# An empty first turn and six branches in TensorE's loop of a batched matmul

## The chip, the cores and the metric

One core of one Trainium2 chip. The metric is the device time of one execution in microseconds.

Each ratio is the mean time of one kernel's runs over that of the other's runs of the same rounds, so it is not quite the ratio of the medians quoted beside it.

## The reference

```python
b1, b2, m, k, n = 8, 16, 256, 512, 384      # 128 independent products
x      = randn(b1, b2, m, k)   # float32
weight = randn(b1, b2, k, n)   # float32
out    = np.matmul(x, weight).astype(np.float32)
```

## The kernel before

The 128 batches go in 32 groups of four (`NG = 32`, `G = 4`). Each engine has its own loop, and the loops meet only through counting semaphores. SyncE issues all loads and stores. ScalarE casts x to bf16 and copies results out of PSUM. VectorE casts the weights and copies the transposed x out of PSUM. TensorE transposes x, then multiplies. `BIAS` is added to some counters at the start, so that a wait for an earlier group never asks for a value of zero or less.

```python
XS, WS, OS = 2, 2 * G // D, 4      # two groups of x and of weights in SBUF
BS, TS, WBS = 1, 2, 2 * G
PT, PO = 4, 2                      # PSUM buffers
BIAS = 8

def load(e, t, U, s):              # SyncE; group n
    n = t * U + s
    if not isinstance(n, int) or n >= XS:
        e.wait_ge(x_cast, n + (1 - XS))          # slot of x free
    e.dma_start(x_sb[s % XS][:], ...).then_inc(x_in[s % XS], 16)
    for d in range(G // D):
        ...
        e.wait_ge(w_cast, n * (G * S) + ((d + 1) * D * S - 2 * G * S))
        e.dma_start(w_sb[slot][:], ...).then_inc(w_in[slot], 16)

def multiply(e, t, U, s):          # TensorE; group n
    n = t * U + s
    e.wait_ge(x_cast, n + 1)
    for q in range(T):             # 4 x 4 transposes
        e.wait_ge(t_copied, n * T + (q + 1 - PT + BIAS))
        ... transposes ...
        ins.then_inc(t_made, 1)
    e.wait_ge(w_cast, n * (G * S) + G * S)
    for q in range(T):             # 4 x 32 multiplies
        e.wait_ge(t_copied, n * T + (q + 1 + BIAS))
        e.wait_ge(o_copied, n * T + (q + 1 - PO + BIAS))
        ... multiplies ...
        ins.then_inc(p_made, 1)

@block.tensor
def _(e):
    U = 2
    e.sem_inc(t_made, BIAS)
    e.sem_inc(p_made, BIAS)
    e.wait_ge(id_done, 2)
    with e.Fori(0, NG // U) as t:   # 16 turns of two groups
        for s in range(U):
            multiply(e, t, U, s)
# ... (cut: SyncE's, VectorE's, ScalarE's and GpSimd's programs)
```

## Time and profile before

| | before |
|---|---|
| time, median of 4 runs | 519.98 us (519.65 to 520.08) |
| bytes over HBM | 167.77 MB read, 50.33 MB written |
| DMA rate between 230 and 262 us | 428 GB/s, DMA share 1.01 |
| PE, VectorE, ScalarE busy | 61%, 62%, 41% of the span |

The table is read from below: no engine is busy for two thirds of the time, and the transfers run at one even rate from the second slice of the span to the last but one. The lines that carry this are shown in the prediction. Two more lines are needed to compare with later. The timeline of the kernel before: start in us, duration in us, engine, line, operation, and in brackets the idle time before it and what ended it.

### The profile page before, as it was taken

What the parts mean: (1) busy time and instruction counts of PE and PEld (TensorE: products, weight loads), DVE (VectorE), ACT (ScalarE), POOL (GpSimd) and SP (SyncE); (2) the same over time, 40 slices, a digit from 0 to 9 for tenths busy, and PEclk for the clock granted to TensorE, in tenths of its full rate; (3) what the DMA queues carried; (4) which work ended last, traced back from release to release, by engine and by line L of the source; (5) the groups of instructions that cost most, each with busy time, mean ns of one, the idle gap of its engine ahead of it and who ended that gap; (6) DMA issues with size and microseconds to landing.
All of it is one profiled execution on the core that took longest, in us unless ns stands there. A gap on an engine that the chain in (4) does not pass through costs nothing.

```text
span 518.3 us, 11239 instructions
## 1 busy us (share of the span) xinstructions
PE 315.5 (61%) x4608; PEld 198.8 (38%) x4608; DVE 323.9 (62%) x384; ACT 212.7 (41%) x193; POOL 0.7 (0%) x6
## 2 busy tenths in 40 slices
PE   0686773576655675655756557665567665675653
PEld 0455452343433443433424334343344333443331
DVE  0878867655577555775556765557755577555670
ACT  3065462454234553245542445423454324553242
POOL 0000000000000000000000000000000000000000
PEclk9988788877687778678776877778787868886787
DMA  8999999999999999999999999999999999999995
GB/s 332 431 426 426 427 427 429 430 426 429 430 428 429 431 426 428 428 431 431 425 429 429 430 430 429 427 428 429 430 430 428 426 431 430 429 428 427 428 431 214
DMA packets 18868, 218.16 MB, mean 421 GB/s; under 512 B 2096, under 2 KB 2096, under 8 KB 2608
## 3 DMA queue, kind: packets, MB, share of 16 engines
q1 hardware_dynamic: 18864, 218.11, 99.2%
q8 instruction: 2, 0.03, 0.0%
q14 instruction: 2, 0.02, 0.0%
HBM read 167.77 MB, written 50.33 MB: 421 GB/s over the span
## 4 chain that ended last, share of the span: by engine, by line
DMA 81%; DVE 12%; issue 2%; PE 2%; ACT 1%; SPq 0%; DVEq 0%; ACTq 0%
DMA w_sb<-in_weight_dram 81%; DVE w_bf L148 12%; PE po L181 2%; ACT x_bf L130 0%; DVEq _compat.py:109 0%; SPq L108 0%; ACT out_sb L195 0%; SPq L100 0%; DVE x_t L154 0%; DVEq L143 0%; DVEq L230 0%; SPq L107 0%; ACTq L194 0%; SPq L288 0%; SPq L54 0%
## 5 line engine op out<-in xcount | busy, mean ns | idle before, releaser
L148 DVE CAST w_bf<-w_sb 64x1536 bf16<-64x1536 f32 x256 | 244.5, 955 | 179.4 <-DMA w_sb<-in_weight_dram 166.7
L181 PE MATMUL po<-w_bf,x_t 128*32 128x384 bf16 x4096 | 231.4, 400 | 121.0 <-DVE x_t L154 121.0
L195 ACT COPY out_sb<-po 128x768 f32<-128x768 f32 x128 | 99.2, 802 | 290.2 <-PE po L181 290.2
L181 PEld LDWEIGHTS po<-w_bf,x_t 128*32 128x32 bf16 x4096 | 124.5, 117 | 225.4 <-DVE x_t L154 130.9
L167 PE MATMUL pt<-identity,x_bf 128*128 128x128 f32 x512 | 84.0, 329 | 73.0 <-ACT x_bf L130 73.0
L130 ACT CAST x_bf<-x_sb 128x2048 bf16<-128x2048 f32 x64 | 118.4, 1901 | 6.1 <-DMA x_sb<-in_x_dram 6.1
L167 PEld LDWEIGHTS pt<-identity,x_bf 128*128 128x128 f32 x512 | 74.3, 213 | 84.9 <-issue 84.9
L154 DVE COPY x_t<-pt 128x1024 bf16<-128x1024 bf16 x128 | 79.5, 683 | 1.0
L130 ACT ACT_TABLE_LOAD x1 | 1.3, 1283 | 1.3 <-PEq L237 1.3
masks.py:199 POOL TENSOR_SCALAR_AFFINE_SELECT identity<-identity 128x128 f32<-128x128 f32 x1 | 0.3, 292 | 0.2 <-POOL identity L204 0.2
L204 POOL MEMSET identity<- 128x128 f32 x1 | 0.2, 204 | 0.5 <-SPq L54 0.5
L277 POOL MEMSET const-bfloat16-1.0<- 128x1 bf16 x1 | 0.1, 101 | 0.0
L277 POOL MEMSET const-uint8-127<- 128x1 uint8 x1 | 0.1, 101 | 0.0
L277 POOL MEMSET const-float32-0.0<- 128x1 f32 x1 | 0.1, 98 | 0.2 <-issue 0.2
L277 POOL MEMSET const-float32-1.0<- 128x1 f32 x1 | 0.1, 98 | 0.0
## 6 DMA issues: line engine op xcount, KB each, us to landing
w_sb<-in_weight_dram SPq DMA_DIRECT2D x64, 1536.0 KB, 27.5
x_sb<-in_x_dram SPq DMA_DIRECT2D x32, 2048.0 KB, 25.8
out_dram<-out_sb SPq DMA_DIRECT2D x31, 1536.0 KB, 30.6
out_dram<-out_sb SPq DMA_DIRECT2D x4, 384.0 KB, 3.6
```

Of the source, the lines that this page charges most:

```text
L130: ins = e.copy(out=x_bf[s % BS][:, :, h], in_=x_sb[s % XS][:].rearrange("p r (q s c) -> p r s q c", s=S, c=KO)[:, :, h],)
L148: e.tensor_copy(out=w_bf[(s * G + d * D + a) % WBS][h * HP : (h + 1) * HP], in_=w_sb[slot][a * HP : (a + 1) * HP, h * KO : (h + 1) * KO, : ...
L154: e.tensor_copy(out=x_t[s % TS][:, 2 * q : 2 * q + 2], in_=pt[(s * T + q) % PT][:].bitcast(bf16),).then_inc(t_copied, 1)
L167: ins = e.transpose(pt[(s * T + q) % PT][:, rr, h, :], words[:, 2 * q + rr, h :: KO // 2], identity[:],)
L181: ins = e.matmul(po[(s * T + q) % PO][mine, rr, :N], x_t[s % TS][:, 2 * q + rr, ko // 2, mine, ko % 2], w_bf[(s * G + i) % WBS][:, ko, :], ...
L195: e.copy(out=out_sb[s % OS][:, 2 * q : 2 * q + 2, :], in_=po[(s * T + q) % PO][:, :, :N],).then_inc(o_copied, 1)
L204: e.memset(identity[:], 0.0).then_inc(id_done, 1)
L277: nc = _bacc.Bacc("TRN2", target_bir_lowering=False, num_devices=1)
```

## The change

It looks like a step towards software pipelining: TensorE's body is cut into a part that transposes and two halves that multiply, each under a condition of its own, and the loop gets one more turn at its beginning. Parts of different groups could later be run in one turn. In this step nothing overlaps yet: in turn 0 all six conditions are false, and in turns 1 to 16 all are true. As TensorE's group number is now two too high, the counters that it waits for are raised by two groups (`LEAD`), and the waits of others are shifted by as much.

```diff
-    BIAS = 8
+    BIAS = 16
+    LEAD = 2
 ...
-            e.wait_ge(x_cast, n + (1 - XS))
+            e.wait_ge(x_cast, n + (1 - XS + LEAD))
 ... (the wait for w_cast likewise)
-    def multiply(e, t, U, s):
+    def transpose(e, t, U, s):
 ... (the transposes; their wait shifted by LEAD * T)
+    def multiply(e, t, U, s, q):
 ... (one block q of multiplies; its waits shifted by LEAD * T)
     # VectorE's program
         e.sem_inc(t_copied, BIAS)
+        e.sem_inc(w_cast, LEAD * G * S)
     # TensorE's program
-        e.wait_ge(id_done, 2)
-        with e.Fori(0, NG // U) as t:
+        with e.Fori(0, NG // U + 1) as t:
             for s in range(U):
-                multiply(e, t, U, s)
+                with e.If(t > 0):
+                    if s == 0:
+                        e.wait_ge(id_done, 2)
+                    transpose(e, t, U, s)
+                for h in range(2):
+                    with e.If(t > 0):
+                        for q in range(h * T // 2, (h + 1) * T // 2):
+                            multiply(e, t, U, s, q)
     # ScalarE's program
         e.sem_inc(o_copied, BIAS)
+        e.sem_inc(x_cast, LEAD)
```

More of the change, by code (lines that the diff above doesn't have):

```diff
@@ L106, in load @@
             if not isinstance(n, int) or n >= 2:
-                e.wait_ge(w_cast, n * (G * S) + ((d + 1) * D * S - 2 * G * S))
+                e.wait_ge(w_cast, n * (G * S) + ((d + 1) * D * S + (LEAD - 2) * G * S))
             e.dma_start(
@@ L163, in multiply @@
         for q in range(T):
-            e.wait_ge(t_copied, n * T + (q + 1 - PT + BIAS))
+            e.wait_ge(t_copied, n * T + (q + 1 - PT + BIAS - LEAD * T))
             for rr in range(2):
@@ L172, in multiply @@
             ins.then_inc(t_made, 1)
-        e.wait_ge(w_cast, n * (G * S) + G * S)
-        for q in range(T):
-            e.wait_ge(t_copied, n * T + (q + 1 + BIAS))
-            e.wait_ge(o_copied, n * T + (q + 1 - PO + BIAS))
-            for rr in range(2):
-                for ko in range(KO):
-                    for i in range(G):
-                        mine = slice(i * C, (i + 1) * C)
-                        ins = e.matmul(
-                            po[(s * T + q) % PO][mine, rr, :N],
-                            x_t[s % TS][:, 2 * q + rr, ko // 2, mine, ko % 2],
-                            w_bf[(s * G + i) % WBS][:, ko, :],
-                            start=(ko == 0),
-                            stop=(ko == KO - 1),
-                        )
-            ins.then_inc(p_made, 1)
+    def multiply(e, t, U, s, q):
+        n = t * U + s
+        if q == 0:
+            e.wait_ge(w_cast, n * (G * S) + G * S)
+        e.wait_ge(t_copied, n * T + (q + 1 + BIAS - LEAD * T))
+        e.wait_ge(o_copied, n * T + (q + 1 - PO + BIAS - LEAD * T))
+        for rr in range(2):
+            for ko in range(KO):
+                for i in range(G):
+                    mine = slice(i * C, (i + 1) * C)
+                    ins = e.matmul(
+                        po[(s * T + q) % PO][mine, rr, :N],
+                        x_t[s % TS][:, 2 * q + rr, ko // 2, mine, ko % 2],
+                        w_bf[(s * G + i) % WBS][:, ko, :],
+                        start=(ko == 0),
+                        stop=(ko == KO - 1),
+                    )
+        ins.then_inc(p_made, 1)
     def copy_out(e, t, U, s, q):
```

## The prediction

> **What bounds the kernel now.** I read the page's busy table and its slices first, then the chain of waits, the transfers with their time to landing, the waits of the DMA queue's issuer, and last the timeline of the start, the middle and the end.
>
> ```profile
> span 518.3 us, 11239 instructions
> PE 315.5 (61%) x4608; PEld 198.8 (38%) x4608; DVE 323.9 (62%) x384; ACT 212.7 (41%) x193; POOL 0.7 (0%) x6
> DMA  8999999999999999999999999999999999999995
> HBM read 167.77 MB, written 50.33 MB: 421 GB/s over the span
> DMA 81%; DVE 12%; issue 2%; PE 2%; ACT 1%; SPq 0%; DVEq 0%; ACTq 0%
> ```
>
> No compute engine is busy for two thirds of the span, while the DMA row stands at nine tenths or more in all slices but the first and the last. The chain that ended last is 81% transfer. In the middle (230 to 262 us) the view by stretches gives 428 GB/s at a DMA share of 1.01. The bytes are 167.77 + 50.33 = 218.1 MB; at 428 GB/s they need 509.6 us, and the span is 518.3 us. So some 9 us in the whole kernel are not pure transfer, all at the two ends. The kernel is bound by bytes, and this change moves no byte of data.
>
> How much lateness of TensorE does the transfer stream stand before it runs dry? That is in the time from issue to landing:
>
> ```profile
> w_sb<-in_weight_dram SPq DMA_DIRECT2D x64, 1536.0 KB, 27.5
> x_sb<-in_x_dram SPq DMA_DIRECT2D x32, 2048.0 KB, 25.8
> out_dram<-out_sb SPq DMA_DIRECT2D x31, 1536.0 KB, 30.6
> ```
>
> A load of 1.57 MB takes 3.7 us alone at 428 GB/s, but lands after 27.5 us: the rest is queue ahead of it. An x load finds 25.8 x 0.428 = 11 MB queued, itself included. A group of four batches moves one x load, two weight loads and one store, 2.10 + 2 x 1.57 + 1.57 = 6.8 MB, or 15.9 us. The queue is thus some one and a half groups deep, and an issue that comes late by under some 20 us only shortens the queue (my estimate, from these landing times; I leave 6 us for uneven queues).
>
> The second question is whether compute keeps up per group:
>
> ```profile
> 26.23 3.71 ACT L130 CAST x_bf<-x_sb 128x2048 bf16<-128x2048 f32 x2
> 30.07 2.85 PE L167 MATMUL pt<-identity,x_bf 128*128 128x128 f32 x16 [1.99 <-ACT x_bf L130]
> 32.67 2.48 DVE L154 COPY x_t<-pt 128x1024 bf16<-128x1024 bf16 x4
> 33.41 5.98 PE L181 MATMUL po<-w_bf,x_t 128*32 128x384 bf16 x128 [0.49 <-DVE x_t L154]
> 37.55 3.70 ACT L130 CAST x_bf<-x_sb 128x2048 bf16<-128x2048 f32 x2
> ```
>
> This is the start, where two groups of data are already there. The ring cast, transposes, copies to x_t, multiplies, next cast turned in 37.55 - 26.23 = 11.3 us. Against 15.9 us of transfer per group, the ring has 4.6 us to spare. In the middle that spare time is visible as PE's waits:
>
> ```profile
> PE po L181 <- DVE x_t L154: 121.0, 32, 6.3
> PE pt L167 <- ACT x_bf L130: 73.0, 32, 12.6
> ```
>
> 121.0 / 32 = 3.8 us ahead of the multiplies and 73.0 / 32 = 2.3 us ahead of the transposes in each group. These waits sit exactly where two of the three new branch pairs of a group will stand.
>
> [...] PE's loop goes back after every second group, yet it was in place before its next input, with 1.98 us of idle ahead of it, at odd and even groups alike:
>
> ```profile
> 255.66 3.11 PE L167 MATMUL pt<-identity,x_bf 128*128 128x128 f32 x16 [1.98 <-ACT x_bf L130]
> 272.15 2.66 PE L167 MATMUL pt<-identity,x_bf 128*128 128x128 f32 x16 [1.98 <-ACT x_bf L130]
> ```
>
> Both start 0.13 us after ScalarE's cast ends (251.83 + 3.70 = 255.53, and 268.32 + 3.70 = 272.02). One of the two has the loop's branch before it. [...]
>
> ```profile
> q8 instruction: 2, 0.03, 0.0%
> q14 instruction: 2, 0.02, 0.0%
> ```
>
> Four packets in a span in which PE went back to its loop's head 15 times: going back fetches nothing. [...]
>
> **The change part by part.**
>
> 1. The bias and the two-group lead. Counters start higher, and waits are shifted by the same amount, so each wait is for the same event as before: x_cast and w_cast are raised by 2 groups' worth, t_made and p_made by 16 in place of 8 with their waits following. VectorE and ScalarE get one more semaphore instruction each, before their first data has come (ScalarE's first cast starts at 8.76 us, VectorE's at 12.43 us, both after a DMA wait). On SyncE the built program shows three more register instructions in a turn of four groups, 21 in 7 turns[...], behind a queue some 20 us deep. Cost 0.
>
> 2. The empty first turn. Six taken compare-and-branches and a loop branch[...]. PE starts at about 1.5 us and is first needed at 12.46 us, when ScalarE's first cast ends:
>
> ```profile
> 12.43 7.86 DVE L148 CAST w_bf<-w_sb 64x1536 bf16<-64x1536 f32 x8 [12.43 <-DMA w_sb<-in_weight_dram]
> 12.59 3.69 PE L167 MATMUL pt<-identity,x_bf 128*128 128x128 f32 x16 [12.59 <-ACT x_bf L130]
> ```
>
> So some 11 us are free. Even later, VectorE casts weights until 20.29 us and only then takes the first transposes, which were done at 16.28 us: 4 us more, and after these the queue's 20 us. Cost 0.
>
> 3. The branches in 16 real turns. Six pairs a turn, three a group[...]. Of the three, one stands ahead of the transposes (2.3 us of waiting there), one ahead of the multiplies (3.8 us of waiting), and one between the second and third blocks of multiplies[...]. Against 4.6 us to spare in the ring: cost 0 in the middle.
>
> 4. The tail. After the last weights land at 493.84 us, VectorE's casts, copies, PE, ScalarE and a store follow in series:
>
> ```profile
> 502.57 6.91 PE L181 MATMUL po<-w_bf,x_t 128*32 128x384 bf16 x128 [3.96 <-DVE x_t L154]
> 509.53 0.80 ACT L195 COPY out_sb<-po 128x768 f32<-128x768 f32 x1 [0.50 <-PE po L181]
> ```
>
> There only the middle pair adds[...].
>
> Sum: 0 + 0 + 0 + 0.2 = +0.2 us on 519.9 us.
>
> **The rivals.**
>
> A, fetches by bandwidth. [...] For: the DMA stream is the bound, so bytes count where latency does not. Against: the loop's own branch over the whole body causes no packets now. Chance about 4%.
>
> B, PE becomes the bound. Each branch would have to stall PE for over 4.6 / 3 = 1.5 us in all. At 3 us for one pair, a group takes 11.3 + 9 = 20.3 us and the kernel 32 x 20.3 = 650 us. [...] Against: the same four packets, and that a not-taken compare falls through to the next instruction. Chance about 2%.
>
> C, a gain. The empty turn could bring the body's code in early; the first multiplies took 7.02 us, the second 5.98 us. But VectorE and the transfers hold the end, so nothing of this 1 us reaches it: 519.9 us. The same holds for any change of PE's clock.
>
> **Range and chances.** The centre is 519.9 + 0.2 = 520.1 us. Runs of the kernel before spread from 519.65 to 520.08 us; I take 519.2 as the low end for another chip or day, and 522.0 as the high end, which holds a slow tail and a few fetches, but not rival A in full. Slower by over 2% (530 us) needs rival B: 2 to 3%. Faster by over 2% would need under 509.5 us, as little as the transfers alone take at 428 GB/s: half a per cent.
>
> **What would show it.** Right: the DMA row at nine in all inner slices and 428 GB/s, landing times near 26 to 28 us, PE's first transposes at some 12.6 us, PE's waits for x_t and x_bf smaller by under 0.5 us a group, and PE's busy time unchanged. Step 2 is wrong if the first transposes start well after 12.6 us; rival A if the instruction queues show hundreds of packets; rival B if PE has idle time of microseconds put down to issue ahead of L169 or L186, and the DMA share falls below nine. The prediction as a whole fails if a branch costs PE over 1.5 us each time.

The sum came to 0 + 0 + 0 + 0.2 = +0.2 us, or 520.1 us. The 0.2 us of the tail rested on a branch time alone and was the author's estimate. So did a part of the range's high end (the slow tail and the few fetches). The argument is where the branches stand: ahead of measured waits of 3.8 and 2.3 us a group, before a first input that comes some 11 us after PE's start, and in a ring with 4.6 us to spare. What a branch takes was measured afterwards, below.

## More of the kernel before

```profile
8.76 3.70 ACT L130 CAST x_bf<-x_sb 128x2048 bf16<-128x2048 f32 x2 [6.13 <-DMA x_sb<-in_x_dram]
29.96 0.33 SPq L100 DMA_DIRECT2D x_sb<-in_x_dram  x1
```

The first is ScalarE's first cast, released by the landing of the first x load. The second is the issue of the fourth group's x load, which needs the second cast and so, by way of TensorE, the first transposes.

## The result, and the profile after

| | before | after |
|---|---|---|
| time, median of 4 runs each | 519.98 us | 520.08 us (519.9 to 520.25) |
| ratio | 1 | 1.0004, 95% interval 0.9989 to 1.0019 |
| first cast of x | 8.76 us | 10.01 us |
| first transposes | 12.59 us | 13.84 us |
| last group's multiplies begin | 502.57 us | 502.72 us |

The time is the same. The page of the changed kernel, in the lines that answer to those of before:

```profile
span 518.4 us, 11383 instructions
DMA  8999999999999999999999999999999999999995
q8 instruction: 2, 0.03, 0.0%
q14 instruction: 2, 0.02, 0.0%
w_sb<-in_weight_dram SPq DMA_DIRECT2D x64, 1536.0 KB, 27.5
x_sb<-in_x_dram SPq DMA_DIRECT2D x32, 2048.0 KB, 25.6
```

The DMA row is the same digit for digit, and the instruction queues show as many packets as before (two of them at another time, see below). PE's waits in the view of waits (engine and line, what it waited for, us in total, times, longest) have not become smaller:

```profile
PE po L186 <- DVE x_t L156: 121.2, 32, 4.9
PE pt L169 <- ACT x_bf L132: 74.2, 32, 13.8
```

121.0 us became 121.2, and 73.0 became 74.2. The 1.2 us more are the first wait alone, 13.8 us in place of 12.6. The branches thus took no time even from TensorE's idle time that this view would show: the sequencer ran them while the engine still worked or waited.

The branches themselves are in the trace, as instructions of PE's sequencer. The view by line gives their number and their durations in ns (least, median, greatest). L248 is the condition ahead of the transposes, L253 the two ahead of the multiplies:

```profile
L248 PEldq COMPARE_BRANCH  x34: 67/68/223, 1.6 to 492.1; - x34
L253 PEldq COMPARE_BRANCH  x68: 67/68/5796, 1.9 to 505.6; - x68
```

34 + 68 = 102 = 6 x 17: only the compares are there. The unconditional branches at the ends of the bodies, which the built program lists, left no record of their own. In the 16 real turns a compare takes 67 or 68 ns, the first of them 77. The greatest value on L253, 5796 ns, is the surprise. Here are all branches of the empty turn, read from the trace's records (start in us, duration in ns):

```
1.553   223   L248  over the transposes, first group
1.894   202   L253  over multiplies 0 and 1
2.154   332   L253  over multiplies 2 and 3
2.544   212   L248  over the transposes, second group
2.814  5796   L253  over multiplies 0 and 1
8.668   217   L253  over multiplies 2 and 3
9.045   219   L246  back to the head of the loop
```

Six of the seven took 0.20 to 0.33 us, and one took 5.8 us. The empty turn lasted from 1.55 to 9.3 us. TensorE was then ready and waited for the first cast:

```profile
10.01 3.70 ACT L132 CAST x_bf<-x_sb 128x2048 bf16<-128x2048 f32 x2 [7.31 <-DMA x_sb<-in_x_dram]
13.84 3.68 PE L169 MATMUL pt<-identity,x_bf 128*128 128x128 f32 x16 [13.84 <-ACT x_bf L132]
```

That cast comes 1.25 us later than in the kernel before, and not because of TensorE, but because the first x load landed later. A load is shared out to sixteen DMA engines and has sixteen landings. In the trace they are, for the first x load:

```
before                        7.86 to 8.74 us, all sixteen
after                         8.03 to 8.92 us, fifteen of them; the last at 9.99 us
the branchless kernel below   7.86 to 8.68 us, all sixteen
```

One engine of sixteen was late. The trace shows why. The view of the transfers of the changed kernel's first 13 us holds a line that the same view of the kernel before lacks:

```profile
q8 instruction: 2, 0.03, 0.9%
```

These are the two packets of queue q8 that the whole page counts in either kernel. By the trace's records of single packets, each is of 16,384 bytes. In the kernel before they ran at 28.35 and 37.87 us; the changed kernel had them at 6.27 and 11.99 us, the first of them while the jump stalled. It took 0.93 us. In these records each packet of an engine begins within some 15 ns of the end of the one before it, so the engine of the fetch can be followed: its next packet of x took 1.11 us in place of the usual 0.61, and it was the last to finish its share of the first x load, at 9.5 us, where the other fifteen had finished by 8.6 us. So the stalled jump fetched one block of 16 KB, and this fetch made the landing late. The same can be followed in the other nine kernels with an empty turn and loads beside it. All ten kernels with an empty turn and loads beside it had the first cast at 9.76 to 10.23 us; the three without an empty turn (before, the branchless one, and the lean one before) had it at 8.70 to 9.03 us.

### The profile page after: what moved, and what is told of

The parts are those of the page before. It is cut to its first block, busy times and chain, and to the rows that moved or that the text cites. A ratio compares the mean times of both kernels' runs of the same rounds, so it can differ in the third digit from the quotient of the medians.

```text
span 518.4 us, 11383 instructions
## 1 busy us (share of the span) xinstructions
PE 314.6 (61%) x4608; PEld 200.7 (39%) x4608; DVE 323.9 (62%) x384; ACT 212.7 (41%) x193; POOL 0.7 (0%) x6
## 4 chain that ended last, share of the span: by engine, by line
DMA 80%; DVE 12%; issue 2%; PE 2%; ACT 1%; SPq 0%; DVEq 0%; ACTq 0%
DMA w_sb<-in_weight_dram 80%; DVE w_bf L150 12%; PE po L186 2%; ACT x_bf L132 0%; DVEq _compat.py:109 0%; SPq L110 0%; ACT out_sb L200 0%; SPq L102 0%; DVE x_t L156 0%; DVEq L145 0%; DVEq L236 0%; SPq L109 0%; DVEq L155 0%; ACTq L199 0%; SPq L302 0%
## 5 line engine op out<-in xcount | busy, mean ns | idle before, releaser
L186 PE MATMUL po<-w_bf,x_t 128*32 128x384 bf16 x4096 | 232.0, 400 | 121.2 <-DVE x_t L156 121.2
L186 PEld LDWEIGHTS po<-w_bf,x_t 128*32 128x32 bf16 x4096 | 127.4, 116 | 222.8 <-issue 184.5
L169 PE MATMUL pt<-identity,x_bf 128*128 128x128 f32 x512 | 82.6, 325 | 74.2 <-ACT x_bf L132 74.2
```

The source lines that it names most:

```text
L169: ins = e.transpose(pt[(s * T + q) % PT][:, rr, h, :], words[:, 2 * q + rr, h :: KO // 2], identity[:],)
L186: ins = e.matmul(po[(s * T + q) % PO][mine, rr, :N], x_t[s % TS][:, 2 * q + rr, ko // 2, mine, ko % 2], w_bf[(s * G + i) % WBS][:, ko, :], ...
```

## The experiments

### How late may TensorE be at the start? (turns5, turns9, turns17, turns13)

Edit, with 5, 9, 13 or 17 for `EMPTY`:

```diff
-    BIAS = 16
-    LEAD = 2
+    EMPTY = 9
+    BIAS = 8 + 8 * EMPTY
+    LEAD = 2 * EMPTY
 ...
-        with e.Fori(0, NG // U + 1) as t:
+        with e.Fori(0, NG // U + EMPTY) as t:
 ...
-                with e.If(t > 0):
+                with e.If(t > EMPTY - 1):
```

> Five empty turns instead of one. In the changed kernel the empty turn took from 1.55 to 9.32 us, of which one jump stalled 5.80 us; without that stall a turn is some 2.0 us (six jumps of 0.20 to 0.33 us with gaps, and the loop's branch). So TensorE should be ready at 9.3 + 4 x 2.0 = 17.3 us, some 3.5 us after the first cast of x ends (13.7 us), and the later turns should show no stall[...]. Theory P (the prediction: lateness at the start is free up to 4 us at VectorE plus a queue of 20 us): time unchanged, 520. Theory S (the queue at the start is shorter, see the run with nine turns; free up to a start of about 21.7 us): 520 as well. Theory F (every taken jump stalls anew by microseconds): turns of 7 us each, a start at 37 us.

> Nine empty turns: TensorE ready at about 9.3 + 8 x 2.0 = 25.3 us. Theory P: the free lateness ends at about 12.5 + 4 + 20 = 36.6 us, so 520. Theory S: at the start only the loads of the first three groups can be issued without TensorE's work (15.7 MB, 36.7 us at 428 GB/s, so the queue runs dry at about 39 us); the fourth group's x load needs the second cast, which ended 17.4 us after TensorE's first transposes in the profile of before (29.93 against 12.59 us). So the free start ends at about 39 - 17.4 = 21.7 us, and nine turns cost 25.3 - 21.7 = 3.6 us: 523.7.

> Seventeen empty turns: TensorE ready at about 9.3 + 16 x 2.0 = 41.3 us. Theory P: 41.3 - 36.6 = 5 us over, 525. Theory S: 41.3 - 21.7 = 20 us over, 540. In both the DMA row should show a hole of that length near 40 us, and nine tenths everywhere after it.

These three ran together. Two theories stood against each other: P, the prediction's, that start lateness is free up to about 36.6 us, and S, that the queue at the start is shorter than in the middle. After they had run, S was mended and tested by a fourth:

> A test of the theory as mended by the runs with 9 and 17 turns. With nine, the first transposes started at 26.31 us and nothing was lost; with seventeen, at 42.86 us, 16.6 us were lost. The fourth group's x load was issued 10.9 and 11.4 us after the first transposes, not 17.4 us as theory S had it, since VectorE and ScalarE had done their part by then. Loss = start - 26.3 us. Thirteen turns start at 42.86 - 4 x 2.07 = 34.6 us: a loss of 8.3 us, 528.2. Theory P (free up to 36.6 us): 520.

Kernels are compared only within the same rounds. Measured; the loss is against the median of before:

| empty turns | first transposes, us | fourth group's x load issued, us | time, us | loss, us |
|---|---|---|---|---|
| 1 (the change) | 13.84 | 31.05 | 520.08 | 0.1 |
| 5 | 18.08 | 29.60 | 519.73 | -0.2 |
| 9 | 26.31 | 37.18 | 520.12 | 0.2 |
| 13 | 34.29 | 45.51 | 528.35 | 8.4 |
| 17 | 42.86 | 54.27 | 536.51 | 16.6 |

Later empty turns took 2.06 to 2.10 us each, with no stall in any of them. Theory F fell. Theory S, which expected 523.7 us for nine turns and 540 for seventeen, was too strict.

The free time ends at a start of some 26 us (42.86 - 16.6 = 26.3, and 34.29 - 8.4 = 25.9); beyond it each microsecond costs one. That is 13.5 us after the kernel before's 12.59 us, not the 24 us of theory P. The mended theory foretold 528.2 us for thirteen turns, and 528.35 us came. The hole is seen in the page of seventeen turns, in slices of 13.4 us:

```profile
DMA  8990899999999999999999999999999999999995
GB/s 332 431 410 5 346 412 424 429 431 430 424 429 430 428 431 430 423 431 428 430 433 426 428 428 430 430 428 430 429 425 430 431 428 433 427 427 429 429 429 229
```

The transfers stop in the fourth slice, and are at full rate again from the seventh on. The reason is in the issues of that kernel, here in the timeline of SyncE's queue:

```profile
13.95 0.33 SPq L103 DMA_DIRECT2D x_sb<-in_x_dram  x1
17.86 4.27 SPq L111 DMA_DIRECT2D w_sb<-in_weight_dram  x2
54.27 0.33 SPq L103 DMA_DIRECT2D x_sb<-in_x_dram  x1
```

Up to 22 us the loads of three groups are issued, 15.7 MB or 36.7 us of transfer, so the queue is empty at about 39 us. The fourth group's x load must wait for the second cast, and that for TensorE. It was issued 11 us after the first transposes, where theory S had taken 17.4 us from the kernel before. 39 - 11 = 28 us. Of the 2 us to the measured 26, one is a load's own time to its first data: by the packet records, the transfers of this kernel stood still from 41.65 to 55.24 us, and the issue was at 54.27 us. The other is not accounted for (the rate falls off before the hole and climbs after it).

### The branchless kernel (ifs_only)

```diff
-    LEAD = 2
+    LEAD = 0
-        with e.Fori(0, NG // U + 1) as t:
+        with e.Fori(0, NG // U) as t:
-                with e.If(t > 0):
+                with e.If(t < NG):
```

(The two extra counter increments are taken out too.)

> The branches without the empty turn: the loop has its 16 turns, the condition is always true, no counter is raised by two groups. 96 compare-and-branches that fall through, no jump is taken. Prediction: 520, equal to both kernels within 0.2%. In the trace, the branches should be 67 to 68 ns each, no stall of microseconds should appear, and the first transposes should start when the first cast of x ends. If the 1.25 us by which the first x load landed later in the changed kernel's profile (first cast at 10.01 against 8.76 us) comes of the empty turn's fetch, the first cast starts near 8.8 us here; if it scatters from run to run, it may stand anywhere between.

519.78 us (519.69 to 519.99), ratio 0.9997 (0.998 to 1.0014). But this was not the experiment that was meant. A loop index that runs from 0 to 15 is always under 32, so the conditions were decided when the program was built; the trace holds no compare on their lines, only the loop's own 16. What ran was the cut of the body and the bias alone. It is of use all the same: with no empty turn, the first cast started at 8.70 us and the sixteen landings lay together. Its two packets of q8 ran at 28.81 and 37.70 us, as late as in the kernel before. So the late landing belongs to the empty turn, not to the bias; and as the first casts of the two groups of kernels above don't overlap, it isn't scatter either.

### The stall by itself (stall_alone)

```diff
     # SyncE's program
+        e.wait_ge(turned, 1)
         for n in range(LAG):
             load(e, 0, NG, n)
     # TensorE's program, at the end of each turn
+            e.sem_inc(turned, 1)
```

> All loads wait until TensorE's empty turn is over, so that its fetch of instructions finds the DMA engines idle. In the changed kernel the fifth jump stalled 5.80 us, and one of the sixteen landings of the first x load came 1.3 us after the others. If the fetch queues behind the loads, [...] the sixteen landings should lie together as in the kernel before. If it is a fixed cost, 5.8 us again. The kernel's time should grow by the wait, 3 to 8 us, as every load starts later.

(How long the stall alone would be was a guess; the test was whether it is shorter than 5.8 us or the same.)

The view by line of the second and third conditions:

```profile
L255 PEldq COMPARE_BRANCH  x68: 67/68/2936, 1.9 to 511.1; - x68
```

The same jump stalled 2.94 us, where ten kernels with loads beside it showed 5.56 to 6.02 us. So about half of the stall is waiting behind the loads. The packet records say the same (us; the packet is q8's first):

```
               jump begins   packet begins, lasts   jump ends
after          2.81          6.27   0.93            8.61
stall_alone    2.81          3.23   1.11            5.74
```

With idle engines the packet began 0.42 us after the jump, with loads beside it 3.46 us after; from its end to the jump's end it was 1.41 us in both. The single run took 525.65 us (state unknown), 5.7 us over before, as every load starts 5.2 us later (first issue at 6.16 in place of 0.97 us). One landing of the first load was still 0.44 us behind the others. The second packet of q8 ran then, from 6.48 to 7.47 us, and the load's first packets began at 7.19 us; but the lean kernel before, below, has a landing 0.48 us late with no fetch near it, so this small delay stays open.

### The changed kernel with the transfers made small (lean_before, lean_after)

The same edit in both kernels. Their outputs are wrong, which doesn't matter for the times.

```diff
+        first = isinstance(n, int) and n < XS
+        RX, KW = (R, S * KO) if first else (R // 4, S * KO // 4)
-            x_sb[s % XS][:],
+            x_sb[s % XS][:, :RX],
 ... (the sources and the weights' loads likewise, with KW)
-                        out=w_bf[...][h * HP : (h + 1) * HP],
+                        out=w_bf[...][h * HP : (h + 1) * HP, :1],
 ... (its source likewise; w_bf is cleared once at the start)
```

> The kernel before with less for the DMA engines and VectorE to do (wrong results on purpose): after the first two groups only a quarter of each x and weight load is moved, and of each weight cast only a quarter is written. A group then moves 0.52 + 0.79 + 1.57 = 2.9 MB, 6.7 us at 428 GB/s, and VectorE needs about 2.5 us for x_t and some 3 us for the casts. What is left as the bound is the ring of cast, transposes, x_t, multiplies, whose turn with data at hand took 9.5 to 11.3 us in the profiles so far. Expected: 32 x 9.5 to 11.3 us plus some 20 us at the ends, 325 to 380 us, with the DMA row well under nine tenths. If the kernel before were bound by compute after all, it would stay near 520.

> The changed kernel, made lean in the same way, so that what its branches cost is no longer hidden by transfers. Measured so far: a branch that falls through takes 67 to 68 ns and some 0.06 us to the next; the first multiplies start 0.08 us later after x_t than before (0.82 against 0.74 us). [...] My expectation now: the branches ahead of the transposes and ahead of the multiplies lie in waits that the ring has in any case, so 0.1 us a group, 3 us, plus 1.3 us at the start: 3 to 6 us over the lean kernel before (1 to 1.5%). [...]

The 9.5 us, which the first of these two expects as the ring's turn, are the time from transposes to transposes with nine empty turns, 37.30 to 46.83 us. VectorE's two figures came out as 2.48 us for x_t and 3.06 us for the casts of a group.

The lean kernel before took 353.19 us (ratio 0.6786, 0.6764 to 0.6808), the lean changed one 351.81 us (0.6767, 0.6754 to 0.6779). Lines of the lean kernel before, the transfers and the shares of the chain of waits:

```profile
DMA packets 18868, 100.20 MB, mean 285 GB/s; under 512 B 2096, under 2 KB 2096, under 8 KB 14128
PE 51%; ACT 23%; issue 16%; DMA 7%; SPq 1%; ACTq 1%; DVE 0%; DVEq 0%
```

Now the transfers have room, and the ring of cast, transposes and multiplies is the bound. Even so the changed kernel is not slower; the intervals overlap, so the 0.3% in its favour isn't counted. I had expected 3 to 6 us. Over 22 groups in the middle the transposes started 10.22 us apart in the one (72.39 to 297.26 us) and 10.24 us in the other (69.94 to 295.14 us); the granted clocks of the two profiled runs were 0.909 and 0.922. The branches cost nothing that these runs can show, even where nothing hides them but the engine's own queue. An example from the changed kernel's trace: the compare ahead of the first multiplies ran at 14.29 us, while the transposes ahead of it were busy from 13.84 to 17.5 us.

### A load on the ring, first attempt (ring16, ring40)

```diff
         e.wait_ge(t_copied, n * T + (q + 1 + BIAS - LEAD * T))
+        if q == 0:
+            for _ in range(40):                # or 16
+                with e.If(t > 2 * NG):
+                    e.wait_ge(id_done, 2)
         e.wait_ge(o_copied, ...)
```

> Sixteen more branches in each group, inside the ring: between the wait for the first x_t and the first multiply, each jumping over one wait that is never run. A taken jump took 0.202 to 0.215 us with 0.06 us to the next, so 16 x 0.27 = 4.3 us a group. The prediction gave the ring 4.6 us to spare in a group; the ring's turn, 9.5 to 11.3 us, becomes 13.8 to 15.6 us, still under 15.9 us. Expected: 520, the same, though TensorE is made to wait 4.3 x 32 = 137 us in all.

> The same with forty: 10.7 us a group. The ring's turn becomes 20.2 to 22.0 us and passes the transfers' 15.9 us, so PE's chain becomes the bound. By the prediction's 11.3 us: 520 + 32 x (10.7 - 4.6) = 715. By the 9.5 us that later profiles show: 520 + 32 x (10.7 - 6.4) = 658. The DMA row should fall to seven or eight tenths.

520.22 us and 520.41 us. These are failed experiments: again the condition could be decided in the build, and the view by line shows one jump a group, of 169 ns, in place of sixteen or forty:

```profile
L183 PEldq COMPARE_BRANCH  x32: 169/169/174, 22.4 to 502.6; - x32
```

Taken at their word they would have told that ten microseconds in the ring are free, which is wrong by 200 us, as the next pair shows.

### A load on the ring (ring16b, ring40b)

```diff
-                with e.If(t > 2 * NG):
+                with e.If(t > NG // U - 1):    # true in the last turn only
```

> As ring16, whose branches never came to the chip: its condition could be decided when the program was built, and the trace shows one jump of 0.169 us in a group in place of sixteen. Here the condition is true in the last turn only, so the branches stay, and all jump in fifteen of sixteen turns. Sixteen at 0.27 us are 4.3 us a group. The lean kernels, bound by the ring, took (353.2 - 20) / 32 = 10.4 us a group; 10.4 + 4.3 = 14.7 us is under the transfers' 15.9 us. Expected: 520, the same. If the ring's spare time were well under 4.3 us, it would be over 525.

> The same with forty: 10.7 us a group. By the prediction's ring of 11.3 us: 32 x (11.3 + 10.7) + 20 = 724. By the lean kernel's 10.4 us: 32 x 21.1 + 20 = 695[...]. The DMA row should fall to seven or eight tenths and the chain of waits should lose its DMA share.

The branches are there now: sixteen turns of two groups make 512 compares for sixteen and 1280 for forty. The other 32 and 80 records, of 169 ns each, stand at the ends of the bodies that ran in the last turn.

```profile
L183 PEldq COMPARE_BRANCH  x544: 65/202/213, 22.3 to 512.9; - x182
L183 PEldq COMPARE_BRANCH  x1360: 65/202/225, 22.6 to 703.7; - x195
```

With forty: 717.77 us, ratio 1.3801 (1.3778 to 1.3824). One jump takes 0.26 us to the next, 10.4 us a group. In the timeline the idle time ahead of the multiplies is put down to nothing but issue:

```profile
268.60 8.20 PE L190 MATMUL po<-w_bf,x_t 128*32 128x384 bf16 x128 [9.02 <-issue]
```

Over 27 groups in the middle, the transposes started from 64.65 to 641.40 us: (641.40 - 64.65) / 27 = 21.4 us a group. Less 10.4 us, the ring's own turn is 11.0 us, where the prediction had 11.3 and the lean kernels 10.2. The granted clock was 0.71 here and 0.91 to 0.92 there; whether that makes the difference was not tested.

With sixteen: 528.79 us, ratio 1.0176 (1.0159 to 1.0193), against an expected 520. In the middle the load is free, as foretold: between 81.54 and 188.16 us the ring turned seven times, in 15.2 us each, under the transfers' 15.9 us. The margin was nearly used up: DMA has 22% of this kernel's chain of waits, where it had 81% before. The page shows the transfers at full rate but for the slices near 60 us and the last two:

```profile
GB/s 335 430 427 417 382 422 428 431 427 426 430 427 431 430 426 425 428 429 429 433 425 428 430 428 431 430 426 429 429 430 427 432 425 428 431 431 428 429 348 128
```

The loss is at the ends, which I had left out. In the last turn the branches fall through, 16 x 0.35 = 5.6 us (the kernel with forty has 13.67 us of issue at its end, 0.34 us each), and this stands in the series that sets the end:

```profile
505.90 2.72 PE L169 MATMUL pt<-identity,x_bf 128*128 128x128 f32 x16 [2.00 <-ACT x_bf L132]
513.22 7.48 PE L190 MATMUL po<-w_bf,x_t 128*32 128x384 bf16 x128 [4.59 <-issue]
```

The last multiplies start at 513.22 us, not at 502.57. The other 5 us come with the last weights, whose casts began at 498.43 us in place of 493.93. The small hole near 60 us, where the queue is still short, accounts for some 1.4 us of these (an estimate from that slice: 46 of 428 GB/s over 13.1 us); what delayed them further was not traced.

## Why the prediction was right, step by step

**The bound.** Right. The transfers set the time as long as TensorE's ring stays under 15.9 us a group; the lean pair shows what the ring alone would take (353 us, at a granted clock of 0.91 in place of 0.79).

**Step 1, bias and lead: 0.** Right: the branchless kernel has the bias and the cut of the body, and is at 0.9997. The lead was not run by itself; it stands in the changed kernel, at 1.0004.

**Step 2, the empty turn: 0.** The cost was right, but its working was not. First, the turn took 7.8 us, of which one jump of seven stalled for 5.8 us. That fits into the 11 us counted as free. Second, TensorE was ready in time (9.3 us), but the cast that was to need it at 12.46 us ended at 13.71 us: the first transposes were to start at some 12.6 us and started at 13.84 us, because the first x load landed 1.25 us later. The prediction had not counted that one packet of 16 KB, on one engine of sixteen, would hold up the first load. Third, "after these the queue's 20 us" was wrong: a depth measured in the middle was used for the start. Altogether 13.5 us are free there, not 24. The change used 1.25 us of them, so the miss didn't show in the time; with thirteen empty turns it would have been a miss of 8 us.

**Step 3, branches in real turns: 0.** Right: a fall-through takes 0.067 us, the unconditional branches left no record, and even the ring-bound lean kernel doesn't feel them. The ring's spare time, 15.9 - 11.3 = 4.6 us, was the term on which all hung; the run with forty jumps gives 15.9 - 11.0 = 4.9 us, the lean kernels 15.9 - 10.2 = 5.7 us. One reading was too high: the 2.3 us ahead of the transposes in each group count the first wait of 12.6 us in; without it they are (73.0 - 12.6) / 31 = 1.95 us, which is the 1.98 us of the timeline. Nothing hung on it.

**Step 4, the tail: +0.2 us.** In the two profiles, the last multiplies started 0.15 us later (502.72 against 502.57), and the spans are 518.4 and 518.3 us. That is consistent with the term, whose size was an estimate, and within the scatter of runs. By the timelines, the first multiplies came 0.82 us after the start of the x_t copies (501.90), where before it was 0.75 us (501.82); one more register operation stands there now.

**Rivals.** A fell: the instruction queues show as many packets as before, four. B fell: no stall after the empty turn, in any of 16 turns. C, a gain through code fetched early: the code did come early (6.27 and 11.99 us in place of 28.35 and 37.87), but the first multiplies took 6.75 us and the second 5.71, still 1.04 us apart as before (7.02 and 5.98). So there was no gain, even ahead of the end.

Still open: why one jump of the seven has to fetch and the others don't, the last microsecond in the account of the free start, and a part of what sixteen extra jumps cost at the end.

## What to carry to other kernels

Ask of an added cost how late its engine may be, and measure that in the place where the cost falls: a queue some 26 us deep in the middle of this kernel left TensorE 13.5 us at the start, and nothing at the end. Branches that ran while their engine still worked or waited were nearly free here: 67 or 68 ns each where they fell through, and 10.24 against 10.22 us a group in the lean pair. But one jump of the empty turn, beside which the instruction queue moved a packet of 16 KB, took 2.9 to 6.0 us (with forty more branches in each group there were two such stalls, of 5.78 and 5.56 us), and in the changed kernel this packet held up one engine's share of the first load, so that the first cast came 1.25 us later. Look for such fetches in time, not only in number: the page of the whole kernel counted the same packets before and after. Before believing that an added load "costs nothing", count its instructions in the trace: three of the kernels here never ran what they were built to test.
